# Up projection of an encoder layer: three seven-product row pairs per group in places three, five and seven, and TensorE in source order

## Chip, cores and metric

The kernel runs on one core of a Trainium2 chip, launched once. The metric is the device time of that core in microseconds (us). An execution's span, from its first to its last instruction in the profile, is given beside it.

Engines are named as in the profile: PE is TensorE (PEld its weight loads), DVE VectorE, ACT ScalarE, POOL GpSimd, SP SyncE. Each takes its own instructions in the order of its queue.

## What is computed

One layer of an encoder on 256 tokens of width 2048, in fp32. Two attention branches are gated, mixed and projected; then comes an MLP, and the change lies in its first half:

```
h = rms_norm(x, norm_mlp_pre)
u = square(relu(h @ w_up))        # 256 x 8192
x = x + rms_norm(u @ w_down, norm_mlp_post)
```

## The kernel before

Every fp32 operand is split into a high part, cast to the type fp32r, and a low part, the difference. A product of two such operands takes three matmuls: high by high, high by low, low by high.

The up projection goes over 8 groups of 1024 columns of `w_up`, u0 to u7 (the loop at L1141 and `wide_group`, L751). A group adds up 8 row pairs: pair i holds rows 256i to 256i + 255 of `w_up`, one load of 1 MB per group and pair (L651). The 256 tokens, the two halves of 128 rows of the pair and the two column halves make a product of 2 by 2 blocks. A plain pair computes it with eight block products, 24 matmuls of 128x512 (`eight`, L736). A heavy pair (`seven`, L724) uses a scheme of seven products, as Strassen's is, 21 matmuls. For that it needs sums of its weight blocks, t0 and t1 (DVE, L660 to L662), their high parts eh0 and eh1 (ACT, L672) and low parts el0 and el1 (DVE, L673), beside the split of three of its four blocks (h on ACT, L659, and l on DVE, L663). A plain pair has one cast of 2048 columns (ACT, L654) and one subtraction (DVE, L656). A heavy pair also needs sums of the stationary operand, `h2sum`, made once in group 0, which has plain pairs alone.

The table `UPS` (L1120) sets the order of the pairs in groups 1 to 7 and which are heavy. In this kernel pairs 3 and 5 are, in places four and six. Names tell group and pair: u3_5h is the high part of pair 5 in group 3. `Weights.next` (L687) prepares pairs two ahead of the one that PE works on. Raw, high and low parts have three buffers each, so a cast into one waits until PE has done with the pair three earlier; t0, t1 are in a pool of 27 pages, and the eh and el parts in a pool `mid`.

PSUM has eight banks. Four (the pool mm) hold products 1, 2, 3 and 7 of a group, to which plain pairs add. Four more (ms) go round among two users. The first are the transposes (`u_T`, L1092): the group before left two chunks of 512 columns, which 16 transposes (PE, L1100) turn, chunk by chunk at the second and third step of a group (n = 1, 2), each chunk in two banks, uT..0 and uT..1; ACT squares each bank into pages (L1103). The second are products 0, 4, 6 and 5, begun by a group's first heavy pair, which takes its products in the order 2, 1, 0, 4, 6, 5, 3. Of these, product 6 gets the bank of the odd chunk's uT..0 and product 5 that of its uT..1. The last heavy pair is followed by `combine` (L742), and the last plain pair by `u_piece` (L1114), which adds and applies ReLU and the row scale.

The squared chunks become stationary operands of the down projection (`u_sets`, `act_sets`, L1035): for an even chunk four sums sm (DVE, L1043 to L1046), then casts ah (ACT, L1058) and differences al (DVE, L1059), which POOL's queue writes to DRAM (L1062); for an odd chunk one cast and one difference. This stands at steps n = 6 and 7 of a group, in the last group at n = 1 and 2.

The instructions are put into each engine's queue by a scheduler that simulates the run. A dependence given by hand (`issue_after`) only orders the queues. `in_order` in `wide_group` does that for the matmuls of a group: each follows the one before it in the source. Here it is off in the up projection. `uw.behind` sets the weights prepared next behind the last addition of the group before.

Of the kernel before, what the change touches and what calls it, by code (L numbers as in the profile page):

```python
# [21 lines left out]
DFF = 4 * D  # L22
# [28 lines left out]
def encoder_layer(ctx: ExitStack, tc: tile.TileContext, a, out):  # L51
# [13 lines left out]
    def page(shape, dt, name):  # L65
        return pages.tile(shape, dt, tag="pg", name=name)
# [328 lines left out]
    late = {}  # L395
# [300 lines left out]
    def columns(src, i, c):  # L696
        return src[i * T : (i + 1) * T, c : c + 1024].rearrange("(k p) c -> p k c", p=P)
# [53 lines left out]
    def wide_group(name, kinds, weights, stat7, stat8, mm_banks, z, piece, each=None, turn=None, after={}, in_order=False):  # L751

        any7 = any(s for _, s in kinds)
        pr = Products(name, mm_banks)
        pr.in_order = in_order
        for n, (i, seven) in enumerate(kinds):
            w = weights.next(after)
            if each:  # L760
                each(n)
            if seven:
                final = not any(s for _, s in kinds[n + 1 :])
                pr.seven(partial(stat7, i), w, final)
                if final:
                    pr.combine(z)
                continue
            end = n == len(kinds) - 1
            if turn and n < 2:
                ahead = [*ahead, (i, w)] if n else [(i, w)]  # L770
                for t in range(2) if n else ():
                    for ii, ww in ahead:
                        for which in (2 * t, 2 * t + 1):
                            pr.eight(partial(stat8, ii), ww, which, False)
                    if not t:
                        turn()
                continue
            for which in range(4):
                pr.eight(partial(stat8, i), w, which, end)
                if end:  # L780
                    b, t, half = PLAIN[which]
                    piece(t, half, pr.ps[b], any7)

    def sums_of(p1, p2, name):

        a11, a21, a12, a22 = p1[:, :P], p1[:, P:], p2[:, :P], p2[:, P:]
        s = page([P, 4, P], F32, f"{name}s")
        nc.vector.tensor_sub(s[:, 0], a21, a22)
        nc.vector.tensor_sub(s[:, 1], a11, a21)
        nc.vector.tensor_sub(s[:, 2], s[:, 0], a11)  # L790
        nc.vector.tensor_add(s[:, 3], a12, s[:, 2])
        parts_ = page([P, 2, 4, P], F32R, name)
        nc.scalar.copy(parts_[:, 0], s)
        nc.vector.tensor_sub(parts_[:, 1], s, parts_[:, 0].bitcast(F32))
        return parts_
# [218 lines left out]
    def first_up(n):  # L1014
        for t, c in {2: [(1, 1), (0, 2)], 3: [(1, 2), (0, 3)], 4: [(1, 3)]}.get(n, ()):
            residual_parts(t, c)
        if n == 5:
            for t in range(2):
                mlp_squares(t)
                mlp_scale(t)  # L1020
            for i in range(4):
                kd = dram.tile([P, 1024], F32, name=f"keepx{i}", tag=f"keepx{i}")
                nc.gpsimd.dma_start(kd, x2[i])
                kept["x", i] = kd
# [10 lines left out]
    def act_sets(cg, u):  # L1035


        srcs = []
        if seven_of(cg):
            a11, a21 = u[:, 0:2, :P], u[:, 0:2, P:]  # L1040
            a12, a22 = u[:, 2:4, :P], u[:, 2:4, P:]
            sums = page([P, 4, 2, P], F32, f"sm{cg}")
            nc.vector.tensor_sub(sums[:, 0], a21, a22)  # L1043
            nc.vector.tensor_sub(sums[:, 1], a11, a21)
            nc.vector.tensor_sub(sums[:, 2], sums[:, 0], a11)
            nc.vector.tensor_add(sums[:, 3], a12, sums[:, 2])  # L1046
            own = [(slice(0, 1), a11.unsqueeze(1)),
                   (slice(1, 3), u[:, 2:4].rearrange("p k (t q) -> p t k q", t=2))]
            if cg in FIRST:
                own.append((slice(3, 4), a21.unsqueeze(1)))  # L1050
            srcs = [([P, 1 + len(own), 2, P], own), ([P, 4, 2, P], [(slice(0, 4), sums)])]
        else:
            srcs = [([P, 4, T], [(slice(0, 4), u)])]
        got = []
        for i, (shape, pieces) in enumerate(srcs):
            hi, lo = page(shape, F32R, f"ah{cg}{i}"), page(shape, F32R, f"al{cg}{i}")
            for at, src in pieces:
                nc.scalar.copy(hi[:, at], src)  # L1058
                nc.vector.tensor_sub(lo[:, at], src, hi[:, at].bitcast(F32))  # L1059
            for n, part in (("h", hi), ("l", lo)):  # L1060
                kd = dram.tile(shape, F32, name=f"keep{n}{cg}{i}", tag=f"keep{n}{cg}{i}")
                nc.gpsimd.dma_start(kd, part.bitcast(F32))  # L1062
                kept[cg, i, n] = (shape, kd)
            got.append([hi, lo])
        return got
# [26 lines left out]
    def u_T(cg, z):  # L1092

        u = page([P, 4, T], F32, f"u{cg}")
        for b in range(2):
            pt = bank(f"uT{cg}{b}")
            for j in range(2):
                for t in range(2):
                    c = (b * 2 + j) * P
                    nc.tensor.transpose(  # L1100
                        pt[:, j * T + t * P : j * T + (t + 1) * P], z[t][:, cg % 2, c : c + P], ident
                    )
            nc.scalar.activation(  # L1103
                u[:, b * 2 : b * 2 + 2], pt.rearrange("p (j q) -> p j q", j=2), AF.Square
            )
        return u

    def u_sets(cg, u):

        got = act_sets(cg, u)  # L1110
        if NG - 4 <= cg < NG - 2:
            sets[0, cg] = got
# [4 lines left out]
            uw.behind = nc.vector.tensor_add(zt, zt, ps).ins  # L1117
        nc.scalar.activation(zt, zt if summed else ps, AF.Relu, scale=r2[:, t : t + 1])

    UPS = [(0, 0), (1, 0), (2, 0), (3, 1), (4, 0), (5, 1), (6, 0), (7, 0)]  # L1120
    uw = Weights()
    for g in range(DFF // 1024):
        for i, seven in UPS if g else ALL8:
            uw.ask(columns(a["w_up"], i, g * 1024), f"u{g}_{i}", seven)
    wd = a["w_down"].rearrange("(g h j p) c -> p h g j c", h=2, j=2, p=P)

    blocks = [[NG - 4] + list(range(0, NG - 4, 2)) + [NG - 2], [NG - 2] + list(range(0, NG - 2, 2))]
# [12 lines left out]
    us = {}  # L1140
    for g in range(DFF // 1024):  # L1141
        z = Late(lambda g=g: [page([P, 2, 512], F32, f"u{g}{t}") for t in range(2)])

        def up_each(n, g=g, uz=uz):
            if not g:
                first_up(n)
                if n == 7:
                    for i in (3, 5):
                        f = page([P, 2, T], F32, f"h2f{i}")
                        for k in range(2):  # L1150
                            d = hT2[i][:, k].bitcast(F32)
                            nc.vector.tensor_add(f[:, k], d[:, :T], d[:, T:])
                        h2sum[i] = sums_of(f[:, 0], f[:, 1], f"h2s{i}")
                return
            cg = g * 2 - 3 + n
            if n in (1, 2):
                us[cg] = u_T(cg, uz)
            late = 0 if g == DFF // 1024 - 1 else 5
            if n - late in (1, 2):
                u_sets(cg - late, us[cg - late])  # L1160

        wide_group(
            f"u{g}",
            UPS if g else ALL8,
            uw,
            h2stat7,
            h2stat8,
            (1, 2, 3, 7),
            z,
            partial(u_piece, z=z),  # L1170
            each=up_each,
            turn=None if g else turn_rows,
            after={} if g else {1: tail[1][1], 2: scaled[0]},
        )
        uz = z

# [213 lines left out]
```

## Time and profile before

| what | value |
|---|---|
| time, median of three runs | 1351.32 us (1351.23 to 1351.63) |
| the profiled execution | 1352.06 us |
| its span | 1350.2 us |
| granted PE clock, mean | 0.998 |
| PE busy | 1337.3 us, 99% |
| DVE, ACT busy | 1029.6 us, 76%; 716.0 us, 53% |
| one group of the up projection (group 3) | 44.08 us |

A row of a timeline gives start, duration, engine, line, operation, output and inputs by name with their shapes, the number of instructions in the row, and in brackets the idle time ahead of it with what ended it. A row of the waits gives what waited, for whom, the total, how often and the longest. A row of the windows gives the stretch and its length, then for PE, PEld, DVE, ACT and POOL the busy time and instructions in it, then the granted clock, the DMA share and GB/s.

### The profile page before, as it was taken

The page shows a single profiled execution, that of the slowest core. Times are in us where ns is not written, and L with a number is a line of the kernel's source. Part 1 is how long each engine was busy: PE and PEld are TensorE (multiplying, and loading weights), DVE is VectorE, ACT ScalarE, POOL GpSimd, SP SyncE. Part 2 cuts the span into 40 slices and gives each one's busy share as a digit, 9 for nine tenths or more (in the row PEclk, how much of TensorE's full clock was granted, in tenths as well). Part 3 has the DMA queues.
Part 4 walks back from the last instruction along what each step waited for, and adds up shares of the span by engine and source line. Part 5 has one row for each costly group of instructions (what it writes and reads, how often), then busy time and mean ns, then how long its engine had stood idle before and what let it go on. Part 6 is the DMA issues. An engine that isn't in the chain of part 4 may idle for free.

```text
span 1350.2 us, 16169 instructions
## 1 busy us (share of the span) xinstructions
PE 1337.3 (99%) x6336; PEld 1118.8 (83%) x6336; DVE 1029.6 (76%) x1181; ACT 716.0 (53%) x841; POOL 38.5 (3%) x71
## 2 busy tenths in 40 slices
PE   9999999999999999999999999999999999999997
PEld 7888888888888888888788888888888888888885
DVE  6968866677857886654777788878888888798896
ACT  5755554544644454344575665666555545554552
POOL 0000000000000000000100000000000000000000
PEclk9999999999999999999999999999999999999999
DMA  9874755564556655575666777678799998798994
GB/s 323 278 220 162 204 163 181 184 183 156 189 187 216 218 187 187 198 270 192 216 204 221 250 273 271 231 234 279 265 339 329 364 359 337 276 357 331 363 360 192
DMA packets 116732, 335.85 MB, mean 249 GB/s; under 512 B 16944, under 2 KB 17712, under 8 KB 116656
## 3 DMA queue, kind: packets, MB, share of 16 engines
q1 hardware_dynamic: 97120, 266.12, 58.0%
q10 hardware_dynamic: 12816, 43.01, 8.3%
q0 software_dynamic: 6720, 25.69, 4.8%
q8 instruction: 49, 0.80, 0.2%
q14 instruction: 27, 0.22, 0.0%
HBM read 307.01 MB, written 29.61 MB: 249 GB/s over the span
## 4 chain that ended last, share of the span: by engine, by line
PE 97%; DVE 1%; DMA 1%; ACT 1%; issue 0%; DVEq 0%; POOLq 0%; POOL 0%; SPq 0%; ACTq 0%
PE u L718 25%; PE p L718 24%; PE ga L718 6%; PE gb L718 6%; PE ba L718 3%; PE bb L718 3%; PE qn_p L214 2%; PE kn_p L214 2%; PE y_p L259 2%; PE y_p L258 2%; PE y_p L257 2%; PE ka_p L214 2%; PE qa_p L214 2%; PE qn_p L216 1%; PE kn_p L216 1%; PE vn_p L258 1%
## 5 line engine op out<-in xcount | busy, mean ns | idle before, releaser
L138 DVE TENSOR_TENSOR y_l<-y_w,y_h 128x1024 fp32r<-128x1024 f32 x32 | 37.9, 1222 | 30.9 <-ACT y_h L133 30.9
L133 ACT CAST y_h<-y_w 128x1024 fp32r<-128x1024 f32 x32 | 32.0, 1051 | 40.9 <-PE y_p L259 32.5
L257 PE MATMUL y_p<-y_h,mh 128*128 128x512 f32 x128 | 50.1, 391 | 0.0
L258 PE MATMUL y_p<-y_l,mh 128*128 128x512 f32 x128 | 49.9, 390 | 0.0
L259 PE MATMUL y_p<-y_h,ml 128*128 128x512 f32 x128 | 49.8, 390 | 0.0
L214 PE MATMUL ka_p<-hT,ka_h 128*128 128x512 f32 x128 | 45.5, 399 | 0.6 <-DVE rope_s L284 0.6
L214 PE MATMUL qn_p<-hT,qn_h 128*128 128x512 f32 x128 | 45.8, 399 | 0.0
L214 PE MATMUL qa_p<-hT,qa_h 128*128 128x512 f32 x128 | 44.5, 403 | 0.8 <-DVE hT L298 0.8
L214 PE MATMUL kn_p<-hT,kn_h 128*128 128x512 f32 x128 | 45.3, 397 | 0.0
L718 PE MATMUL u<-u_0h,h2T 128*128 128x512 f32 x128 | 45.0, 396 | 0.0
L718 PE MATMUL u<-u_1h,h2T 128*128 128x512 f32 x128 | 43.7, 396 | 0.0
L718 PE MATMUL u<-u_2h,h2T 128*128 128x512 f32 x128 | 41.8, 396 | 0.0
L718 PE MATMUL u<-u_4h,h2T 128*128 128x512 f32 x128 | 41.2, 391 | 0.0
L718 PE MATMUL u<-u_6h,h2T 128*128 128x512 f32 x128 | 41.0, 389 | 0.0
L718 PE MATMUL u<-u_7h,h2T 128*128 128x512 f32 x128 | 40.9, 389 | 0.0
L656 DVE TENSOR_TENSOR u_7l<-u_7r,u_7h 128x2048 fp32r<-128x2048 f32 x8 | 18.3, 2293 | 28.1 <-ACT u_7h L654 28.1
L216 PE MATMUL qn_p<-hT,qn_l 128*128 128x256 f32 x128 | 35.9, 281 | 0.0
L216 PE MATMUL kn_p<-hT,kn_l 128*128 128x256 f32 x128 | 35.7, 280 | 0.0
L216 PE MATMUL ka_p<-hT,ka_l 128*128 128x256 f32 x128 | 35.2, 280 | 0.0
L216 PE MATMUL qa_p<-hT,qa_l 128*128 128x256 f32 x128 | 33.3, 282 | 0.4 <-DVE qa_l L138 0.3
L654 ACT CAST u_1h<-u_1r 128x2048 fp32r<-128x2048 f32 x8 | 15.3, 1914 | 33.6 <-PE u L718 29.6
L654 ACT CAST u_7h<-u_7r 128x2048 fp32r<-128x2048 f32 x8 | 15.3, 1914 | 31.8 <-issue 26.5
(1387 smaller groups left out, 4374.5 us busy)
## 6 DMA issues: line engine op xcount, KB each, us to landing
y_w<-in_w_out SPq DMA_DIRECT2D x16, 1024.0 KB, 5.1
bh<-keeph ACTq DMA_DIRECT2D x30, 512.0 KB, 9.8
bl<-keepl ACTq DMA_DIRECT2D x30, 512.0 KB, 11.5
keeph<-ah POOLq DMA_DIRECT2D x18, 512.0 KB, 6.3
keepl<-al POOLq DMA_DIRECT2D x18, 512.0 KB, 7.1
va_w<-in_w_in SPq DMA_DIRECT2D x8, 1024.0 KB, 5.1
qn_w<-in_w_in SPq DMA_DIRECT2D x8, 1024.0 KB, 5.1
kn_w<-in_w_in SPq DMA_DIRECT2D x8, 1024.0 KB, 5.1
```

What stands on the lines that cost most here:

```text
L133: nc.scalar.copy(hi[part], raw[part])
L138: sub = nc.vector.tensor_sub(lo[part], raw[part], hi[part].bitcast(F32)).ins
L214: nc.tensor.matmul(ps[b], hi[:, k % 4, cs], mv, start=(k == 0), stop=False)
L216: nc.tensor.matmul(ps[b][:, :T], lo[:, k % 4, cs], mv[:, :T], start=False, stop=(k == nk - 1))
L257: nc.tensor.matmul(ps[t], sh, hi[:, k % 4], start=(k == 0), stop=False)
L258: nc.tensor.matmul(ps[t], sh, lo[:, k % 4], start=False, stop=False)
L259: nc.tensor.matmul(ps[t], sl, hi[:, k % 4], start=False, stop=(k == nk - 1))
L654: nc.scalar.copy(h1, raw)
L656: nc.vector.tensor_sub(l1, raw, h1.bitcast(F32))
L718: ins = nc.tensor.matmul(self.ps[i], st, mv[:, blk], start=i not in self.begun, stop=last and n == 2).ins
```

## The change

Pair 0 becomes heavy too, and the pairs get a new order: 1, 2, 0, 4, 3, 6, 5, 7, with the heavy ones in places three, five and seven. The el parts go into pages instead of `mid`. In groups 1 to 7 PE's matmuls follow the source. The stationary sets move from steps n = 6 and 7 to n = 3 and 5, the fourth and the sixth step; the last group keeps n = 1 and 2. A third h2 sum is made.

```diff
-    UPS = [(0, 0), (1, 0), (2, 0), (3, 1), (4, 0), (5, 1), (6, 0), (7, 0)]
+    UPS = [(1, 0), (2, 0), (0, 1), (4, 0), (3, 1), (6, 0), (5, 1), (7, 0)]
...
-            uw.ask(columns(a["w_up"], i, g * 1024), f"u{g}_{i}", seven)
+            uw.ask(columns(a["w_up"], i, g * 1024), f"u{g}_{i}", seven, page)
...
-                    for i in (3, 5):
+                    for i in (0, 3, 5):
...
-            late = 0 if g == DFF // 1024 - 1 else 5
-            if n - late in (1, 2):
-                u_sets(cg - late, us[cg - late])
+            steps = (3, 5) if g < DFF // 1024 - 1 else (1, 2)
+            if n in steps:
+                cg = g * 2 - 2 + steps.index(n)
+                u_sets(cg, us[cg])
...
+            in_order=g > 0,
```

In the built program PE has 21 fewer matmuls of L718 (3 in each of groups 1 to 7), and as many transposes.

ACT in group 3, around the squares. Before: u4 and u5 are the even and the odd chunk, uT40 to uT51 their banks.

```order
L659 CAST u3_3h_6529<-u3_3r_6527 128x1536 [waits DMAHW7_49,PE_49,Activation_49]
L1103 ACTIVATE u4_6546<-uT40_6547 128x512 [waits PE_49]
L672 CAST u3_3eh1_6542<-u3_3t1_6532 128x1024 [waits DVE_49]
L1103 ACTIVATE u4_6546<-uT41_6553 128x512 [waits PE_49]
L654 CAST u3_4h_6585<-u3_4r_6583 128x2048 [waits DMAHW0_49,PE_49,Activation_49]
L1103 ACTIVATE u5_6589<-uT50_6590 128x512 [waits PE_49]
L1103 ACTIVATE u5_6589<-uT51_6596 128x512 [waits PE_49]
L672 CAST u3_5eh0_6637<-u3_5t0_6630 128x1024 [waits DVE_49]
```

Pair 3 is the first heavy pair here. Between the squares of the two chunks stand one eh cast and the cast of plain pair 4.

The same place after the change; u3_0 is now the first heavy pair, u3_3 the second, u3_6 the plain pair after it:

```order
L672 CAST u3_0eh1_6539<-u3_0t1_6529 128x1024 [waits DVE_49]
L1103 ACTIVATE u4_6577<-uT40_6578 128x512 [waits DMASW4_49,PE_49]
L1103 ACTIVATE u4_6577<-uT41_6584 128x512 [waits PE_49]
L659 CAST u3_3h_6616<-u3_3r_6614 128x1536 [waits DMAHW0_49,PE_49,Activation_49]
L672 CAST u3_3eh0_6625<-u3_3t0_6618 128x1024 [waits DVE_49]
L672 CAST u3_3eh1_6629<-u3_3t1_6619 128x1024 [waits DVE_49]
L654 CAST u3_6h_6673<-u3_6r_6671 128x2048 [waits DMAHW1_49,PE_49,Activation_49]
L1103 ACTIVATE u5_6633<-uT50_6634 128x512
L1103 ACTIVATE u5_6633<-uT51_6640 128x512
```

The squares of the odd chunk, u5, moved behind all three casts of u3_3 and that of u3_6.

PE in group 3 after the change, in the first heavy pair; u30, u34, u36 and u35 are products 0, 4, 6 and 5 of group 3:

```order
L718 MATMUL u30_6652<-u3_0h_6526,h2T0_4813 128x512 [waits Activation_49]
L718 MATMUL u30_6652<-u3_0l_6527,h2T0_4813 128x512
L718 MATMUL u30_6652<-u3_0h_6526,h2T0_4813 128x512
L718 MATMUL u34_6656<-u3_0eh0_6535,h2s0_5769 128x512 [waits Activation_49]
L718 MATMUL u34_6656<-u3_0el0_6536,h2s0_5769 128x512 [waits DVE_49]
L718 MATMUL u34_6656<-u3_0eh0_6535,h2s0_5769 128x512
L718 MATMUL u36_6660<-u3_0eh0_6535,h2s0_5769 128x512 [waits PE_49,Activation_49]
L718 MATMUL u36_6660<-u3_0el0_6536,h2s0_5769 128x512
L718 MATMUL u36_6660<-u3_0eh0_6535,h2s0_5769 128x512
L718 MATMUL u35_6664<-u3_0eh1_6539,h2s0_5769 128x512 [waits PE_49,Activation_49]
L718 MATMUL u35_6664<-u3_0el1_6540,h2s0_5769 128x512 [waits DVE_49]
L718 MATMUL u35_6664<-u3_0eh1_6539,h2s0_5769 128x512
```

Product 6 waits for ACT (the square of uT50, as the bank's user before it), as the 13th matmul after the last transpose; all later matmuls of the pair stand behind it. Before, plain pair 2 stood between the transposes and the first heavy pair.

ACT in group 1 after the change, around the squares of u1, the odd chunk:

```order
L672 CAST u1_3eh0_5925<-u1_3t0_5918 128x1024 [waits DVE_49]
L672 CAST u1_3eh1_5929<-u1_3t1_5919 128x1024 [waits DVE_49]
L659 CAST u1_3h_5916<-u1_3r_5914 128x1536 [waits DMAHW0_49,PE_49,Activation_49]
L1103 ACTIVATE u1_5933<-uT10_5934 128x512 [waits PE_49]
L1103 ACTIVATE u1_5933<-uT11_5940 128x512 [waits PE_49]
L1058 CAST ah00_5982<-u0_5877 128x256 [waits Activation_49]
L1058 CAST ah00_5982<-u0_5877 128x512 [waits Activation_49]
L654 CAST u1_6h_5973<-u1_6r_5971 128x2048 [waits DMAHW1_49,PE_49]
```

Here both eh casts of the second heavy pair stand ahead of u1_3h, and the squares ahead of u1_6h.

Group 7, the last, where the sets are made at the second and third step. Before, on PE, at the end of plain pair 4 (the place after the first heavy pair, u7_3); u76, u75 and u73 are products 6, 5 and 3:

```order
L718 MATMUL u73_7873<-u7_4h_7970,h2T4_4817 128x512 x2
L718 MATMUL u73_7873<-u7_4l_7971,h2T4_4817 128x512
L718 MATMUL u76_8052<-u7_3eh0_7898,h2s3_5769 128x512 [waits PE_49,Activation_49]
L718 MATMUL u76_8052<-u7_3el0_7899,h2s3_5769 128x512
L718 MATMUL u76_8052<-u7_3eh0_7898,h2s3_5769 128x512
L718 MATMUL u75_8056<-u7_3eh1_7902,h2s3_5769 128x512 [waits PE_49,Activation_49]
L718 MATMUL u75_8056<-u7_3el1_7903,h2s3_5769 128x512
L718 MATMUL u75_8056<-u7_3eh1_7902,h2s3_5769 128x512
L718 MATMUL u73_7873<-u7_4h_7970,h2T4_4817 128x512
```

Products 6 and 5 of heavy pair 3 had been put behind nearly all of plain pair 4; in the changed program they stand in their own pair, as in group 3.

After the change, on ACT, from the squares of chunk 12 (even) to those of chunk 13 (odd):

```order
L1103 ACTIVATE u12_7977<-uT120_7978 128x512 [waits PE_49]
L1103 ACTIVATE u12_7977<-uT121_7984 128x512 [waits PE_49]
L1058 CAST ah120_7995<-u12_7977 128x256 [waits Activation_49]
L1058 CAST ah120_7995<-u12_7977 128x512 [waits Activation_49]
L1058 CAST ah120_7995<-u12_7977 128x256
L659 CAST u7_3h_8041<-u7_3r_8039 128x1536 [waits DMAHW0_49,PE_49]
L654 CAST u7_6h_8106<-u7_6r_8104 128x2048 [waits DMAHW1_49,PE_49]
L1058 CAST ah121_8007<-sm12_7990 128x1024 [waits DVE_49]
L672 CAST u7_3eh0_8050<-u7_3t0_8043 128x1024 [waits DVE_49]
L672 CAST u7_3eh1_8054<-u7_3t1_8044 128x1024 [waits DVE_49]
L1103 ACTIVATE u13_8058<-uT130_8059 128x512
L1103 ACTIVATE u13_8058<-uT131_8065 128x512
```

The squares of uT130 and uT131 now stand behind the ah casts of chunk 12, u7_3h, u7_6h and both eh casts.

After the change, on DVE, at the same place:

```order
L663 TENSOR_TENSOR u7_3l_8042<-u7_3r_8039,u7_3h_8041 128x1536 [waits DMAHW0_49,Activation_49]
L1046 TENSOR_TENSOR sm12_7990<-u12_7977,sm12_7990 128x256 [waits DVE_49]
L656 TENSOR_TENSOR u7_6l_8107<-u7_6r_8104,u7_6h_8106 128x2048 [waits DMAHW1_49,Activation_49]
L1059 TENSOR_TENSOR al121_8008<-sm12_7990,ah121_8007 128x1024 [waits Activation_49]
L660 TENSOR_TENSOR u7_3t0_8043<-u7_3r_8039 128x1024 [waits DMASW6_49]
L661 TENSOR_TENSOR u7_3t1_8044<-u7_3t0_8043,u7_3r_8039 128x512 [waits DVE_49]
L662 TENSOR_TENSOR u7_3t1_8044<-u7_3t1_8044,u7_3r_8039 128x512 [waits DVE_49]
L673 TENSOR_TENSOR u7_3el0_8051<-u7_3t0_8043,u7_3eh0_8050 128x1024 [waits DMASW7_49,Activation_49]
L673 TENSOR_TENSOR u7_3el1_8055<-u7_3t1_8044,u7_3eh1_8054 128x1024 [waits Activation_49]
L1059 TENSOR_TENSOR al130_8072<-u13_8058,ah130_8071 128x1024 [waits Activation_49]
```

The sums t0 and t1 of u7_3, from which ACT casts eh0 and eh1, stand behind u7_6l and al121.

## Prediction

> **What bounds the kernel now.** I read the page's first and fourth parts, then the list of waits on TensorE (PE) from 640 us to the end, then one whole group of the up projection (group 3) in the windows and the timeline.
>
> ```profile
> span 1350.2 us, 16169 instructions
> PE 1337.3 (99%) x6336; PEld 1118.8 (83%) x6336; DVE 1029.6 (76%) x1181; ACT 716.0 (53%) x841; POOL 38.5 (3%) x71
> PE 97%; DVE 1%; DMA 1%; ACT 1%; issue 0%; DVEq 0%; POOLq 0%; POOL 0%; SPq 0%; ACTq 0%
> PE u L718 <- DVE u_1l L656: 0.8, 1, 0.8
> 788.58:832.66 44.08, 44.08 (x203) 36.48 (x202) 35.71 (x35) 25.94 (x26) 3.23 (x7) 1.00 0.75 257
> ```
>
> PE is busy for 99% of the span and makes 97% of the chain that ends last. The fourth row is all that PE waits from 640 us on: one wait of 0.8, in group 0. The fifth is group 3 from its first matmul to that of group 4: 44.08 us, PE busy in all of it, DVE for 35.71, ACT for 25.94, granted clock 1.00. So a matmul saved here is time saved, and a wait added is time added, with nothing on PE to hide it.
>
> ```profile
> 811.59 0.39 PE L718 MATMUL u<-u_4h,h2T 128*128 128x512 f32 x1
> 817.03 0.39 PE L718 MATMUL u<-u_5h,h2s 128*128 128x512 f32 x1
> 821.79 0.39 PE L718 MATMUL u<-u_6h,h2T 128*128 128x512 f32 x1
> ```
>
> These are the first matmuls of a plain pair, of the heavy pair behind it and of the next plain pair. Matmuls overlap, so their cost is the distance of starts: 24 take 817.03 − 811.59 = 5.44, 21 take 4.76, 0.2267 each. Group 3 has 6 × 24 + 2 × 21 = 186 matmuls, 42.17; the 16 transposes take the other 44.08 − 42.17 = 1.91.
>
> **The change part by part.** *Matmuls removed.* A third heavy pair takes 3 matmuls from each of groups 1 to 7: 21 × 0.2267 = 4.76 us, all of it on the path.
>
> *What the third heavy pair adds on DVE and ACT.* Beside a plain pair it adds these and drops one cast and one subtraction:
>
> ```profile
> 817.27 1.91 ACT L654 CAST u_7h<-u_7r 128x2048 fp32r<-128x2048 f32 x1 [5.29 <-issue]
> 819.22 2.29 DVE L656 TENSOR_TENSOR u_7l<-u_7r,u_7h 128x2048 fp32r<-128x2048 f32 x1 [4.40 <-ACT u_7h L654]
> 808.59 1.76 DVE L663 TENSOR_TENSOR u_5l<-u_5r,u_5h 128x1536 fp32r<-128x1536 f32 x1 [1.67 <-ACT u_5h L659]
> 991.21 1.22 DVE L660 TENSOR_TENSOR u_5t<-u_5r 128x1024 f32<-128x1024 f32 x1
> 992.47 0.69 DVE L661 TENSOR_TENSOR u_5t<-u_5t,u_5r 128x512 f32<-128x512 f32 x1
> 993.19 0.69 DVE L662 TENSOR_TENSOR u_5t<-u_5t,u_5r 128x512 f32<-128x512 f32 x1
> 993.80 1.22 DVE L673 TENSOR_TENSOR u_5el<-u_5t,u_5eh 128x1024 fp32r<-128x1024 f32 x1
> ```
>
> DVE: 1.76 + 1.22 + 2 × 0.69 + 2 × 1.22 − 2.29 = 4.5 more, 40.2 of a group's 43.4 without waits. ACT gains one cast of 1.48 and two of 1.05 (rows below) and loses 1.91: 27.6. Both fit, so I cost them at nothing; what it costs where the cover fails is the fourth rival. The third h2 sum is made once, in group 0, and the low parts in pages take the same time in another buffer.
>
> *The places and the order.* Here lies the cost. The transposes of the group before (uT) take the four ms banks of PSUM, two at each of the second and third steps, and ACT's squares (L1103) empty them. The next users are products 0, 4, 6, 5 of the group's first heavy pair, so product 6 waits for the square of the third step's first bank. Before, this pair is the fourth, and a plain pair lies between. Now it is third: its product 6 stands 12 matmuls behind the last transpose, and as PE's order is that of the source, whatever it waits for stops all that follows.
>
> How late is that square? The order of ACT (in the part on the change) puts it behind u3_3h, two eh casts and u3_6h. The times come from these rows:
>
> ```profile
> 797.37 0.40 PE L718 MATMUL u<-u_0h,h2T 128*128 128x512 f32 x1
> 797.85 1.48 ACT L659 CAST u_3h<-u_3r 128x1536 fp32r<-128x1536 f32 x1 [3.98 <-PE u L718]
> 799.23 0.59 ACT L1103 ACTIVATE u<-uT 128x512 f32<-128x512 f32 x1
> 799.72 1.04 ACT L672 CAST u_3eh<-u_3t 128x1024 fp32r<-128x1024 f32 x1
> 800.66 0.60 ACT L1103 ACTIVATE u<-uT 128x512 f32<-128x512 f32 x1
> 801.15 1.91 ACT L654 CAST u_4h<-u_4r 128x2048 fp32r<-128x2048 f32 x1
> 802.95 1.09 ACT L1103 ACTIVATE u<-uT 128x512 f32<-128x512 f32 x2
> ```
>
> u_3h's cast waits for the last matmul that reads the buffer it goes into, and starts 0.48 behind that matmul's start. From start to start the casts take 1.38 (L659), 0.94 (L672) and 1.80 (L654); a square lasts 0.59.
>
> Groups 2 to 6, clock at 0 with the group's first matmul: two plain pairs and the transposes end at 2 × 5.44 + 1.91 = 12.8, and product 6 is due 12 × 0.2267 later, at 15.52. The last matmul of the second pair, u_2, starts before the eight late transposes: 12.8 − 0.95 − 0.23 = 11.62. ACT starts u3_3h at 12.10 and ends the square at 12.10 + 1.38 + 2 × 0.94 + 1.80 + 0.59 = 17.75. PE follows 0.05 later:
>
> ```profile
> 654.75 2.28 DVE L656 TENSOR_TENSOR u_1l<-u_1r,u_1h 128x2048 fp32r<-128x2048 f32 x1
> 657.08 0.50 PE L718 MATMUL u<-u_1l,h2T 128*128 128x512 f32 x1 [0.85 <-DVE u_1l L656]
> 657.42 0.62 PE L718 MATMUL u<-u_1h,h2T 128*128 128x512 f32 x2
> ```
>
> (654.75 + 2.28 = 657.03, then 657.08.) The wait is 17.80 − 15.52 = 2.28, in five groups 11.4. It is at least 1.85 if the cast follows its matmul at 0.05 instead of 0.48, and at most 3.4 if DVE's sums hold the eh casts for one L660 (1.22) more; I take the 0.48, since that row shows this very wait. The restart costs too: the second matmul came 0.34 after the first instead of 0.227, 0.11 for each wait.
>
> Group 1: the order has ACT's late squares ahead of u1_6h and its eh casts early, so the squares end near 14.4, before 15.5: no wait.
>
> Group 7: the order keeps the sets at the second and third steps. There ACT does the early squares, ah casts, u7_3h, u7_6h, ah, both eh casts and only then the late squares; the second eh cast needs DVE's L662, and that stands behind u7_6l and al121.
>
> ```profile
> 1024.43 1.22 DVE L1059 TENSOR_TENSOR al<-sm,ah 128x1024 fp32r<-128x1024 f32 x1
> 1025.57 1.22 DVE L660 TENSOR_TENSOR d000t<-d000r 128x1024 f32<-128x1024 f32 x1
> 811.40 2.29 DVE L656 TENSOR_TENSOR u_6l<-u_6r,u_6h 128x2048 fp32r<-128x2048 f32 x1
> 813.60 1.22 DVE L673 TENSOR_TENSOR u_5el<-u_5t,u_5eh 128x1024 fp32r<-128x1024 f32 x1
> ```
>
> u7_6h takes the buffer of u7_0h, read last by the heavy pair's ninth matmul, which starts at 12.8 + 8 × 0.2267 = 14.61; so ACT starts it at 15.09 and it ends at 17.00. DVE starts u7_6l 0.04 later, as 819.22 follows 817.27 + 1.91. Then 2.20 (start to start, 811.40 to 813.60) and 1.14 for al121 (1024.43 to 1025.57) end at 20.38. L660 and L661 take 1.26 and 0.72 (991.21, 992.47, 993.19), L662 0.69: 23.05. ACT's second eh cast follows at 23.10, the square at 24.04, ending 24.63; PE goes on at 24.68. Product 6 was due at 15.52: a wait of 9.16.
>
> That PE used to have the freedom that the change takes away can be seen in group 7 of before, where the squares end at 984.95 + 1.08 = 986.03:
>
> ```profile
> 984.95 1.08 ACT L1103 ACTIVATE u<-uT 128x512 f32<-128x512 f32 x2
> 985.88 0.39 PE L718 MATMUL u<-u_3eh,h2T 128*128 128x512 f32 x1
> 990.42 0.39 PE L718 MATMUL u<-u_3eh,h2s 128*128 128x512 f32 x1
> ```
>
> Product 3 was taken at 985.88, and products 6 and 5 only at 990.42, behind most of the next plain pair.
>
> *The sum.* −4.76 + 11.4 + 9.16 + 6 × 0.11 = +16.5. The profiled execution took 1352.06 (its span 1350.2 and 1.86 around it): 1368.6. The median is 0.74 below that execution, so I forecast **1367.8**.
>
> **The rivals.** *The clock.* After the pause of 9 us PE might run slowly for a while. The nearest rows are the kernel's first matmuls and the same form a little later:
>
> ```profile
> 5.51 1.64 PE L214 MATMUL qa_p<-hT,qa_h 128*128 128x512 f32 x4 [0.30 <-DVE hT L298]
> 7.46 1.08 PE L214 MATMUL qa_p<-hT,qa_h 128*128 128x512 f32 x4
> ```
>
> By them it costs 0.56 more: 1368.4. The Trainium skill, "TensorE: Matmul & The Clock Gate" (Part 1, and the closing table), says that an idle window of about 3.4 us puts the clock back to half until about 3.4 us of work have passed; by that page I estimate 1.7 more, 1369.5. No run here shows which: the trace has no pause of that length within the work.
>
> *Group 7 waits only as the others do* (DVE makes its sums earlier than the order says): 2.28 in place of 9.16 gives 1360.9. Against it: engines take their rows in order, and L662 stands behind u7_6l.
>
> *The other side: the squares come in time.* If ACT reached them by 15.5 − 5.65 = 9.8 instead of 12.10, that is if u_3h's buffer came free a pair earlier, no wait is left, only the 4.76 saved: 1351.32 − 4.76 = 1346.6. It decides at 2.28 less on ACT's chain in groups 2 to 6. Against it speaks 797.85, where this very cast waits on PE for 3.98.
>
> *DVE becomes the bound.* Its idle time per group before is 44.08 − 35.71 = 8.4. If it is all unavoidable (waits on ACT), a group needs 40.2 + 8.4 = 48.6 instead of the forecast's 44.08 − 0.68 + 2.28 + 0.11 = 45.8: 5 × 2.8 = 14 more, 1382. Against it: much of that idle time is DVE waiting for buffers that PE holds.
>
> That nothing changes can be left out: the order shows 21 matmuls fewer.
>
> **How the numbers follow.** Forecast 0.64, at 1365.6 to 1373.4 (five waits of 1.85 or 3.4); clock 0.15; group 7 like the others 0.10; squares in time 0.07; DVE 0.04. The range goes from 1358.7 (group 7 like the others, with the low waits) to 1373.4. A difference of 0.2%, 2.7 us, is about what a measurement of this kernel can tell from no change. Faster by more: the squares in time, 0.06, and 0.02 within; slower the rest, 0.92.
>
> **What would show it.** In the list of waits, matmuls of u that wait for ACT's squares, L1103: five times about 2.3 and once about 9.2. Group windows of about 45.8 (groups 2 to 6), 43.4 (group 1) and 52.7 (group 7), with the clock at 1.00. The down projection as long as before. I am wrong if the product behind the eh matmuls of the first heavy pair follows at 0.23, or if PE waits for DVE's el parts rather than for ACT.

## The result and the profile after

The changed kernel took 1377.28 us (median of 4 runs, 1376.14 to 1377.45) against 1351.47 before: 25.8 us slower; over all runs the ratio is 1.0186 (95% interval 1.0173 to 1.0199). The forecast was 1367.8 with a range to 1373.4, so the direction was right, the size too small, and the time lies above the range. The profiled execution took 1377.42, its span 1375.6.

The page of the changed kernel, and below it all waits of PE from 640 us on:

```profile
span 1375.6 us, 16212 instructions
PE 1342.9 (98%) x6315; PEld 1121.9 (82%) x6315; DVE 1060.9 (77%) x1223; ACT 727.1 (53%) x856; POOL 38.5 (3%) x71
PE 95%; ACT 2%; DVE 1%; DMA 1%; SPq 0%; issue 0%; DVEq 0%; POOLq 0%; POOL 0%; ACTq 0%
```

```profile
PE u L718 <- ACT u L1103: 19.7, 6, 8.9
PE u L718 <- DVE u_1l L656: 0.8, 1, 0.8
```

The six forecast waits for ACT's squares are there, 19.7 us in all, and no other wait is new. They account for most of the loss but not for all of it. And PE is busy for 5.6 us *more* than before, 1342.9 against 1337.3, though it has 21 matmuls fewer. Something made matmuls longer. The six places in the timeline of PE:

```profile
761.64 0.50 PE L718 MATMUL u<-u_0eh,h2s 128*128 128x512 f32 x1 [2.15 <-ACT u L1103]
807.46 0.50 PE L718 MATMUL u<-u_0eh,h2s 128*128 128x512 f32 x1 [2.16 <-ACT u L1103]
854.89 0.51 PE L718 MATMUL u<-u_0eh,h2s 128*128 128x512 f32 x1 [2.16 <-ACT u L1103]
902.34 0.50 PE L718 MATMUL u<-u_0eh,h2s 128*128 128x512 f32 x1 [2.15 <-ACT u L1103]
949.76 0.50 PE L718 MATMUL u<-u_0eh,h2s 128*128 128x512 f32 x1 [2.16 <-ACT u L1103]
1003.97 0.80 PE L718 MATMUL u<-u_0eh,h2s 128*128 128x512 f32 x1 [8.93 <-ACT u L1103]
```

ACT ahead of the second of them:

```profile
801.74 1.48 ACT L659 CAST u_3h<-u_3r 128x1536 fp32r<-128x1536 f32 x1 [2.55 <-issue]
803.12 2.00 ACT L672 CAST u_3eh<-u_3t 128x1024 fp32r<-128x1024 f32 x2
805.02 1.89 ACT L654 CAST u_6h<-u_6r 128x2048 fp32r<-128x2048 f32 x1
806.82 1.07 ACT L1103 ACTIVATE u<-uT 128x512 f32<-128x512 f32 x2
```

The two squares, in one row here, stand behind the four casts, and PE goes on at 807.46, 17.79 after the group's start at 789.67 (forecast: 17.80).

The waits are equal in groups 2 to 6, but the stretches between them are not: 45.82 from the first to the second, then 47.43, 47.45, 47.42. The windows of the groups say where that comes from (groups 2, 3, 4, 7 and the down projection; after the busy times comes the granted clock):

```profile
743.85:789.67 45.82, 43.66 (x201) 35.91 (x199) 39.89 (x41) 27.30 (x27) 3.23 (x6) 1.00 0.71 246
789.67:837.10 47.43, 45.27 (x200) 37.04 (x199) 39.85 (x41) 27.32 (x27) 3.23 (x6) 0.96 0.68 240
837.10:884.55 47.45, 45.29 (x201) 37.06 (x199) 39.86 (x41) 27.30 (x27) 3.23 (x6) 0.96 0.68 239
...
979.40:1034.46 55.06, 46.13 (x200) 37.70 (x199) 40.67 (x42) 28.20 (x28) 3.19 (x6) 0.91 0.64 225
1034.46:1375.60 341.14, 331.86 (x1472) 274.68 (x1470) 281.00 (x250) 171.68 (x146) 4.60 (x8) 0.99 0.85 326
```

Group 2 ran at a clock of 1.00, groups 3 to 6 at 0.96, group 7 at 0.91. In group 3, right behind the pause:

```profile
807.80 0.55 PE L718 MATMUL u<-u_0el,h2s 128*128 128x512 f32 x1
808.15 1.05 PE L718 MATMUL u<-u_0eh,h2s 128*128 128x512 f32 x2
809.00 0.63 PE L718 MATMUL u<-u_0el,h2s 128*128 128x512 f32 x1
809.43 0.63 PE L718 MATMUL u<-u_0eh,h2s 128*128 128x512 f32 x1
...
810.71 0.63 PE L718 MATMUL u<-u_0eh,h2T 128*128 128x512 f32 x1
811.13 0.48 PE L718 MATMUL u<-u_4h,h2T 128*128 128x512 f32 x1
811.45 0.40 PE L718 MATMUL u<-u_4l,h2T 128*128 128x512 f32 x1
```

From start to start a matmul takes 0.43 instead of 0.227, until 811.13, and then it is back. Against a group with the same pause and the full clock (group 2) that costs 47.43 − 45.82 = 1.61.

| part of the sum | forecast | measured |
|---|---|---|
| matmuls saved (group 1: 43.40) | −4.76 | −4.76 |
| waits of groups 2 to 6 | 5 × 2.28 = 11.4 | 5 × 2.16 = 10.8 |
| wait of group 7 | 9.16 | 8.93 |
| restarts | 0.66 | 5 × (45.82 − 43.40 − 2.15) + 0.11 = 1.46 |
| slow clock, groups 3 to 6 | 0 | 4 × 1.61 = 6.44 |
| slow clock, group 7 | 0 (as a rival 0.56) | 55.06 − 43.40 − 8.93 − 0.11 = 2.62 |
| down projection | 0 | 341.14 − 341.20 = −0.06 |
| sum | 16.5 | 25.4 |

The last column meets the difference of the spans, 1375.6 − 1350.2 = 25.4.

The row of the restarts holds more than a restart. The forecast counted a wait from the time when the product was due to start, the profile counts idle time from the end of the matmul before. A matmul starts 0.227 after the one before it but lasts 0.39, so the profile's wait is 0.16 shorter. In the forecast's terms the waits were 2.32 and 9.09, and the matmul behind a wait came 0.11 late, both nearly as forecast. The same 0.16 is in the 2.62 of group 7, which leaves 2.46 for the clock there.

### The profile page after: what moved, and what is told of

It is laid out like the page before. It is cut to its first block, busy times and chain, and to the rows that moved or that the text cites. A ratio compares the mean times of both kernels' runs of the same rounds, so it can differ in the third digit from the quotient of the medians.

```text
span 1375.6 us, 16212 instructions
## 1 busy us (share of the span) xinstructions
PE 1342.9 (98%) x6315; PEld 1121.9 (82%) x6315; DVE 1060.9 (77%) x1223; ACT 727.1 (53%) x856; POOL 38.5 (3%) x71
## 4 chain that ended last, share of the span: by engine, by line
PE 95%; ACT 2%; DVE 1%; DMA 1%; SPq 0%; issue 0%; DVEq 0%; POOLq 0%; POOL 0%; ACTq 0%
PE u L718 25%; PE p L718 24%; PE ga L718 6%; PE gb L718 6%; PE ba L718 3%; PE bb L718 3%; PE ka_p L214 2%; PE qn_p L214 2%; PE kn_p L214 2%; PE y_p L258 2%; PE y_p L259 2%; PE y_p L257 2%; PE qa_p L214 1%; PE qn_p L216 1%; PE ka_p L216 1%; PE kn_p L216 1%
## 5 line engine op out<-in xcount | busy, mean ns | idle before, releaser
L718 PE MATMUL u<-u_2h,h2T 128*128 128x512 f32 x128 | 43.4, 401 | 0.0
L718 PE MATMUL u<-u_4h,h2T 128*128 128x512 f32 x128 | 43.3, 408 | 0.0
L718 PE MATMUL u<-u_1h,h2T 128*128 128x512 f32 x128 | 41.4, 392 | 0.0
L718 PE MATMUL u<-u_6h,h2T 128*128 128x512 f32 x128 | 40.7, 390 | 0.0
L718 PE MATMUL u<-u_7h,h2T 128*128 128x512 f32 x128 | 40.7, 389 | 0.0
L718 PE MATMUL u<-u_0eh,h2s 128*128 128x512 f32 x42 | 18.2, 467 | 19.7 <-ACT u L1103 19.7
L1118 ACT ACTIVATE u<-u,r 128x512 f32<-128x512 f32 x32 | 21.5, 713 | 28.3 <-DVE u L1117 26.8
L656 DVE TENSOR_TENSOR u_1l<-u_1r,u_1h 128x2048 fp32r<-128x2048 f32 x8 | 18.3, 2290 | 20.3 <-ACT u_1h L654 20.3
L718 PEld LDWEIGHTS u<-u_4h,h2T 128*128 128x128 f32 x128 | 25.9, 203 | 5.8
```

What stands on the lines that cost most here:

```text
L656: nc.vector.tensor_sub(l1, raw, h1.bitcast(F32))
L718: ins = nc.tensor.matmul(self.ps[i], st, mv[:, blk], start=i not in self.begun, stop=last and n == 2).ins
```

## The experiments

Two things were to be told apart: whether PE's waits come from ACT's queue as the order has it, and whether the slow matmuls come from the pauses or from something else that three heavy pairs bring (DVE at 40 us per group). Unless something else is said, an edit is made to the changed kernel. Times are medians; each is set against runs of the kernel before on the same chip.

**Only the squares' place on ACT** (sq_first). The names between u2_6 and u6_6 are left out here. The added lines shift later ones by three: L721 and L1106 are L718 and L1103.

```diff
+    last_sq = [None]
...
-            nc.scalar.copy(h1, raw)
+            with tc.issue_after(last_sq[0]) if name in ("u2_6", ..., "u6_6") else nullcontext():
+                nc.scalar.copy(h1, raw)
...
-            nc.scalar.activation(
+            last_sq[0] = nc.scalar.activation(
                 u[:, b * 2 : b * 2 + 2], pt.rearrange("p (j q) -> p j q", j=2), AF.Square
-            )
+            ).ins
```

> The changed kernel with one thing moved on ACT: in groups 2 to 6 the cast of the plain pair 6 (L654) is put behind the odd chunk's two squares. Theory (PE waits for the squares as ACT's queue has them, and the clock falls where over about 1.75 us of a window of 3.4 us are idle): the squares come 1.80 sooner, the five waits fall from 2.16 to 0.36, the clock stays up in these groups, each takes 44.0, and the time is 1377.3 - 5 x 1.80 - 4 x 1.61 = 1361.9, with group 7 as it was. Rival (the wait is for something else that ends at the same time, such as u_6's cast or el1 on DVE): waits of 2.2 stay, 1377. Rival (the clock is lowered by a wait of any length): 1368.

Measured: 1361.96 (ratio to before 1.0078, 1.0064 to 1.0092). Ahead of product 6 only the cast u_6h moved, behind the squares; farther on in the group u_7h also moved, ahead of the eh casts of u_5, without a wait of PE. PE's waits:

```profile
759.21 0.50 PE L721 MATMUL u<-u_0eh,h2s 128*128 128x512 f32 x1 [0.35 <-ACT u L1106]
803.22 0.50 PE L721 MATMUL u<-u_0eh,h2s 128*128 128x512 f32 x1 [0.36 <-ACT u L1106]
...
987.84 0.79 PE L721 MATMUL u<-u_0eh,h2s 128*128 128x512 f32 x1 [8.93 <-ACT u L1106]
```

The waits are 1.80 shorter, which is one cast of 2048 columns, and groups 2 to 6 take 44.0 each. Both the wait's cause and the sum of wait and clock stand as the theory had them.

**Work in place of the pause** (fill). Groups 2 to 6 compute product 4 of the first heavy pair three more times, to no use.

```diff
+            if 4 not in self.begun and self.name in ("u2", "u3", "u4", "u5", "u6"):
+                for _ in range(3):
+                    self.add(4, stat(3), t[0], 0, True)
+                    self.begun.discard(4)
             self.add(4, stat(3), t[0], 0, last)
```

> In groups 2 to 6 the first heavy pair computes its product 4 four times (three times to no use), 9 more matmuls, 2.04 us, ahead of product 6; so PE works through most of its pause of 2.16. Theory (the slow clock comes from the pause): no slow matmuls in these groups, each 45.7 us, about 6.5 us less in all though nothing is saved: 1370 to 1371. Rival (matmuls there are slow for another reason, such as what ACT and DVE do at that time): groups of 47.4 as now, 1377.

Measured: 1371.53 (1.0142, 1.0128 to 1.0156), though PE has 45 matmuls more. Two of its groups:

```profile
744.49:790.30 45.81, 45.69 (x209) 37.58 (x208) 39.89 (x41) 27.32 (x27) 3.22 (x6) 1.00 0.70 245
790.30:836.13 45.83, 45.70 (x209) 37.58 (x208) 39.85 (x41) 27.33 (x27) 3.23 (x6) 1.00 0.71 249
```

Groups 3 to 6 fell from 47.43 to 45.83, the clock is 1.00, and DVE and ACT are as busy as they were (39.9 and 27.3). So it is the pause that lowers the clock, not the load beside it.

**A shorter pause** (p3_first).

```diff
-            self.add(6, stat(4), t[0], 1, last)
-            self.add(5, stat(5), t[1], 0, last)
-            self.add(3, stat(2), t[1], 1)
+            if self.name[0] == "u":
+                self.add(3, stat(2), t[1], 1)
+            self.add(6, stat(4), t[0], 1, last)
+            self.add(5, stat(5), t[1], 0, last)
+            if self.name[0] != "u":
+                self.add(3, stat(2), t[1], 1)
```

> Product 3 is put ahead of products 6 and 5, so these are due 0.68 later, and the pauses are 1.48 in groups 2 to 6 and 8.25 in group 7. Theory (the clock is lowered where about 1.9 us or more of a window of 3.4 us are idle): the short pauses leave the clock at 1.00, groups 2 to 6 take 45.1, and the time is 1377.3 - 6 x 0.68 - 4 x 1.63 = 1366.7. Rival (any pause costs the clock some 1.6 us in four groups of five): 1373.2. Rival (slow clock in proportion to the pause): 1371.

Measured: 1367.37 (1.0112, 1.0098 to 1.0125). The five pauses for the squares (L1106 here) are 1.48 and cost no clock; a group is 45.13:

```profile
761.42 0.50 PE L718 MATMUL u<-u_0eh,h2s 128*128 128x512 f32 x1 [1.48 <-ACT u L1106]
806.54 0.50 PE L718 MATMUL u<-u_0eh,h2s 128*128 128x512 f32 x1 [1.48 <-ACT u L1106]
```

0.68 less of waiting saved 2.3 in each of groups 3 to 6. A cost in proportion to the pause is out, and so is a cost of any pause.

**Group 7's sets later** (sets7).

```diff
-            steps = (3, 5) if g < DFF // 1024 - 1 else (1, 2)
+            steps = (3, 5)
```

> The changed kernel, with the sets of the last group at the fourth and sixth step as in the others. Theory (the long wait of group 7 is u7_6l and al121 standing ahead of the sums on DVE): ACT's order becomes that of groups 2 to 6, the wait there falls from 8.9 to 2.2, group 7 takes 47.4 (45.8 if the clock stays up) in place of 55.1, and the time is 1377.3 - 7.6 = 1369.7 (1368.1). Rival (the sets, now later, hold up the start of the down projection): group 7 shorter, but a wait of PE for ah or al at its first matmuls, 1372 or more.

Measured: 1369.87 (1.0133, 1.0119 to 1.0147). The wait of group 7 falls from 8.93 to that of the others, and the group takes 47.41:

```profile
951.67 0.50 PE L718 MATMUL u<-u_0eh,h2s 128*128 128x512 f32 x1 [2.16 <-ACT u L1103]
997.48 0.60 PE L718 MATMUL u<-u_0eh,h2s 128*128 128x512 f32 x1 [2.16 <-ACT u L1103]
```

So the early sets of the last group are what made its wait long. The down projection was hardly held up by the later ones: its only wait is 0.2 us, on a load of a kept low part. This run also has six equal pauses, of which five were followed by slow matmuls (all but that of 951.67).

**Source order alone, in the kernel before** (b_inorder).

```diff
             after={} if g else {1: tail[1][1], 2: scaled[0]},
+            in_order=g > 0,
```

> The kernel before with in_order in groups 1 to 7 and nothing else. Theory (source order costs only where a matmul is late, and a plain pair stands between the transposes and the first heavy pair here): no more than 0.3 us in group 7, 1351 to 1353. Rival (source order costs in itself, by taking from PE the filling of small gaps): 1355 or more, spread over all groups.

Measured: 1354.72 against 1351.81 (1.0023, 1.0014 to 1.0032). Neither theory had this. Groups 1 to 6 take 44.0 to 44.1 as before, so nothing is spread; but in group 7 one wait came up:

```profile
998.81 0.51 PE L718 MATMUL u<-u_5el,h2s 128*128 128x512 f32 x1 [1.84 <-DVE u_5el L673]
```

That is 1.84 and not the 0.3 that I allowed: with PE in source order, the second heavy pair's el part is late there. On ACT and DVE the cast and the subtraction of plain pair u_7 stand ahead of its eh cast and of the el part itself (u_7l from 995.33 for 2.29 us, u_5el from 997.54 for 1.22), and on DVE the sums of u_5 stand behind u_6l and an al of the sets. Which of these matters most was not tried in this kernel. The profiled span is 2.0 longer than that of before; the rest of the 2.9 between medians isn't explained.

**PE's order left to the scheduler** (free_order).

```diff
-            in_order=g > 0,
```

> The changed kernel without in_order in the up projection; the scheduler is free to put products 6 and 5 later. Theory: the squares are as late as they were, but no matmul stands behind them, so PE does not wait in groups 2 to 6, and under 1 us in group 7: 1346.7 to 1347.7. Rival (three heavy pairs cost more in themselves): 1351 or more, with waits on DVE.

Measured: 1351.41 (0.9994, 0.9985 to 1.0003), as the kernel before. Groups 1 to 6 took 43.3 each with no wait: although the squares are behind the same casts, products 6 and 5 stand farther back. Group 7 took 47.43, with a slow stretch at half clock and, ahead of it, two waits that the theory did not have:

```profile
1001.76 0.50 PE L718 MATMUL u<-u_5eh,h2s 128*128 128x512 f32 x1 [0.68 <-ACT u_5eh L672]
1004.28 0.50 PE L718 MATMUL u<-u_5el,h2s 128*128 128x512 f32 x1 [1.79 <-DVE u_5el L673]
```

The time did not reach the 1346.7 that I gave. The next run asks whether the sets of the last group are the reason.

**The two together** (free_sets7): without `in_order`, and `steps = (3, 5)` in every group.

> free_order with the sets of the last group at the fourth and sixth step. Theory: without them ahead, the sums and eh casts of u7_5 come in time, the two waits of 0.7 and 1.8 in group 7 and the slow clock behind them go, and group 7 takes 43.3 in place of 47.4: 4 us less than free_order, 1347.4. Rival (the loss moves on to the start of the down projection): 1351 as free_order.

Measured: 1349.03 (0.9978, 0.9969 to 0.9987), faster than the kernel before. All seven groups take 43.3, so group 7 gave back its 4.2. Of the gain, part went to the rival's place: the down projection is 345.16 long, against 343.55 in free_order and 341.20 in the kernel before, with 2.4 us of waits on loads of kept low parts that the kernel before does not have. The other 1.6 of these 4.0 isn't explained.

```profile
PE p L718 <- DMA bl<-keepl: 2.4, 3, 1.6
```

**Both chunks transposed at the second step** (t_early), in source order.

```diff
-            cg = g * 2 - 3 + n
-            if n in (1, 2):
-                us[cg] = u_T(cg, uz)
+            if n == 1:
+                for cg in (g * 2 - 2, g * 2 - 1):
+                    us[cg] = u_T(cg, uz)
```

> Both chunks are transposed at the second step of a group, so that ACT's squares stand ahead of u3_3h and u3_6h; all else is as in the changed kernel. Theory (all of the loss is PE's wait for the squares and the slow clock behind these pauses): no wait on L1103 is left, groups of 43.4 us, granted clock 1.00, and the time is that of the kernel before less 4.76: 1346.7. Rival (three heavy pairs cost more in themselves, by DVE's 40 us of work per group): PE waits for el parts or sums in place of squares, groups of 44 us or more, 1351 to 1377.

Measured: 1356.64 (1.0032, 1.0021 to 1.0043): a miss for the theory as stated. No wait for squares is left, but in groups 2, 4 and 6 another has come, and one in group 7:

```profile
783.60 0.50 PE L718 MATMUL u<-u_5el,h2s 128*128 128x512 f32 x1 [1.88 <-DVE u_5el L673]
874.12 0.50 PE L718 MATMUL u<-u_5el,h2s 128*128 128x512 f32 x1 [1.88 <-DVE u_5el L673]
963.04 0.50 PE L718 MATMUL u<-u_5el,h2s 128*128 128x512 f32 x1 [1.88 <-DVE u_5el L673]
997.36 0.50 PE L718 MATMUL u<-u_3el,h2s 128*128 128x512 f32 x1 [0.88 <-DVE u_3el L673]
```

ACT and DVE of this run, ahead of the first of these:

```profile
778.17 1.91 ACT L654 CAST u_1h<-u_1r 128x2048 fp32r<-128x2048 f32 x1 [3.61 <-PE u L718]
779.99 1.04 ACT L672 CAST u_5eh<-u_5t 128x1024 fp32r<-128x1024 f32 x1
```

```profile
777.33 0.68 DVE L662 TENSOR_TENSOR u_5t<-u_5t,u_5r 128x512 f32<-128x512 f32 x1
780.12 2.29 DVE L656 TENSOR_TENSOR u_1l<-u_1r,u_1h 128x2048 fp32r<-128x2048 f32 x1 [2.10 <-ACT u_1h L654]
782.33 1.22 DVE L673 TENSOR_TENSOR u_5el<-u_5t,u_5eh 128x1024 fp32r<-128x1024 f32 x1
```

The sum was ready at 778.0; ACT could not cast it, since the next group's u_1h stood ahead of it and waited 3.61 for PE to give a buffer free (and on DVE u_1l stood ahead of u_5el). The first of PE's four waits also lowered the clock: group 2 took 47.24, groups 4 and 6 took 45.7. In groups 3 and 5 the two casts stand the other way round, with no wait and 43.25 per group. This is the first fault again, a cast that waits for PE ahead of one that PE waits for, and not DVE's load.

**That order mended** (early_eh): t_early, `steps = (3, 5)`, and plain pairs' casts behind the last eh cast made before them.

```diff
+    last_eh = [None]
...
-            nc.scalar.copy(h1, raw)
+            with tc.issue_after(last_eh[0]) if last_eh[0] and name[0] == "u" else nullcontext():
+                nc.scalar.copy(h1, raw)
...
-            nc.scalar.copy(h2[i], t[i])
+            last_eh[0] = nc.scalar.copy(h2[i], t[i]).ins
```

> t_early, with plain pairs' casts (L654) put behind the last eh cast of the heavy pair ahead of them, and the sets of the last group at the fourth and sixth step. Theory (what t_early lost in groups 2, 4 and 6 is u_5's second eh cast standing on ACT behind the next group's u_1h, which waits for PE): no waits of 1.9 on u_5el, groups of 43.3, 1346.7 to 1348. Rival (DVE's 40 us per group leave no room, so another el part or sum comes late in its place): 1351 or more.

Measured: 1348.69 (0.9978, 0.9969 to 0.9987). Groups 1 to 7 take 43.3, with no wait of PE in them. Three heavy pairs do fit, then, and the rival on DVE's load falls; the time is a little over the theory's 1348.

**The same with PE's order free** (early_eh_free): without `in_order` as well.

> early_eh with the order of PE left to the scheduler. Theory (no matmul is late there any more, so source order costs nothing): the same groups of 43.3, 1348 to 1349.5, no better than early_eh. Rival (source order costs in itself): 1 us or more less than early_eh, 1347.5 or below.

Measured: 1347.65 (0.9970, 0.9960 to 0.9981), the fastest of all, with the same groups of 43.2 to 43.3 and the same span of 1345.9 as early_eh. The spans say that source order costs nothing there; the medians are 1.0 apart, but come from two different chips, and don't settle it.

## Why the prediction was wrong

*What bounds the kernel, the matmuls saved.* Right: every wait added shows in full, and group 1, the one without a wait, takes 43.40 as forecast.

*The places and the order.* Right in mechanism, place and size: five waits of 2.16 of idle time (2.32 from the due start) against 2.28, one of 8.93 (9.09) against 9.16, and none in group 1. sq_first moved the one cast and the wait went down by its 1.80; sets7 took the sets away and group 7's wait became that of the others.

*What three heavy pairs add on DVE and ACT, at nothing.* Right for this kernel; the busy time is 39.9 and 27.3 against the forecast's 40.2 and 27.6. The cover is thinner than I made it where the order is bad: t_early, free_order and, with two heavy pairs, b_inorder each show an el part that comes 1.8 to 1.9 late.

*The clock.* This is the step that failed: the sum put the clock at nothing behind all six pauses. The prediction had a slow clock as a rival, after the pause of 9 us alone, at 0.56 from the kernel's first matmuls. It came after that pause at 2.62, and after four of the five pauses of 2.2 at 1.61 each: 9.1 us that the sum left out, and without which it would have been within 0.3 of what was measured (16.5 − 0.85 for shorter waits + 0.8 for longer restarts, against 25.4 − 9.1). For the pauses of 2.2 the prediction gave no reason to put it at nothing. Its one reading was the granted clock of 1.00 in group 3 of the kernel before, and that kernel has no pause over 0.85 from 640 us on, so its profile could say nothing on such pauses.

The Trainium skill, "TensorE: Matmul & The Clock Gate" (Part 1), gave a half clock for about 3.4 us, which I estimated at 1.7, for the pause of 9 us alone. That size agrees with the 1.61 measured behind each of four shorter pauses. Its condition, a whole idle window of about 3.4 us, does not: 2.16 was enough in four groups of five, so the measurement decides.

*The range* ended at 1373.4 since it took in the bounds of the waits and not that of the clock for each of them: five more times 1.6 would have put its upper end at 1381. (A small slip besides: 2.28 + 1.22 is 3.50, not 3.4.)

*The rivals* on group 7, on squares in time and on DVE as the bound did not come.

## What to carry to other kernels

Where PE is the bound and its order is fixed, look on each helper engine's queue for an instruction that waits for PE and stands ahead of one that PE waits for; each such pair can be a stall, and moving one cast took 1.80 away five times. Price a new PE pause at more than its length: here 2.16 of waiting cost up to 2.16 + 0.27 + 1.61, and cutting it to 1.48 saved 2.3 where the clock had fallen. Saved matmuls (4.76) were there all along: with the queues mended the same three heavy pairs came out 3.1 to 4.3 us, 0.2 to 0.3%, faster than the kernel before.

## What the runs showed of the hardware

A pause of PE of about 2 us can halve the granted clock for 3.4 us after it (0.43 per matmul of 128x512 instead of 0.227). Pauses of 1.48 never did (five of five), those of 1.79 to 1.88 in two cases of five (free_order once; t_early in group 2, not in 4 and 6; not in b_inorder), those of 2.16 in nine of eleven (four of five in the changed kernel, five of six in sets7), those of 8.3 to 8.9 in all four runs that were looked at for it, for 10.2 us that begin within the pause.

The slow stretches do not begin at a fixed time behind the pause: 0.44 after it in group 3 of the changed kernel, 1.50 after it in group 6. They keep a grid, which the granted clock of its trace shows. Stretches of groups 3, 4 and 7:

```profile
807.90:811.30 3.40, 3.40 (x10) 2.62 (x9) 3.40 (x5) 0.80 (x2) 0.54 (x1) 0.50 0.77 295
811.31:855.68 44.37, 42.21 (x194) 34.70 (x193) 36.79 (x37) 26.86 (x27) 2.69 (x5) 1.00 0.68 236
855.69:859.09 3.40, 3.40 (x9) 2.65 (x8) 3.40 (x5) 0.45 (x1) 0.54 (x1) 0.50 0.77 266
999.05:1009.28 10.23, 5.31 (x13) 4.16 (x14) 9.26 (x11) 5.17 (x6) 1.59 (x3) 0.50 1.00 354
```

The clock is 0.50 or 1.00 in the whole of each row. The slow stretches of groups 3 to 7 begin at 807.90, 855.68, 903.47, 951.26 and 999.04, each 47.79 after the one before, which is 14 × 3.413; the first four last 3.41, the last 10.24, which is 3 × 3.413. So the clock changed only at the ends of windows of about 3.413 us, wherever PE's pauses lay. By this grid the pause of group 2, 759.48 to 761.64, is cut at 760.11 into 0.63 and 1.53, and no slow stretch followed. That of group 6, 947.60 to 949.76, is cut at 947.84 into 0.24 and 1.92, and the clock fell at that window's end, 951.26. Those of groups 3 to 5 lie whole in one window each.

The two closest cases are the sixth group of sets7 and group 7 of free_order, one window and the next of each:

```profile
949.96:953.36 3.40, 1.69 (x7) 1.42 (x8) 3.40 (x5) 2.96 (x5) 0.15 (x1) 1.00 0.90 296
953.37:956.77 3.40, 3.40 (x16) 2.82 (x15) 2.60 (x5) 0.77 (x1) 0.93 (x2) 1.00 0.72 233
```

```profile
1001.98:1005.38 3.40, 1.61 (x7) 1.00 (x7) 2.50 (x3) 0.21 (x1) 0.00 (x0) 1.00 0.96 373
1005.39:1008.79 3.40, 3.40 (x10) 2.66 (x9) 3.37 (x6) 0.74 (x1) 0.00 (x0) 0.50 1.03 419
```

With 1.72 of a window idle the clock stayed up, with 1.79 it fell. A threshold between these two, on the idle time within one window, gives the outcome of all 21 pauses of 1.48 to 2.16 counted above. That the clock goes by this idle time is an inference from them: pauses of chosen length at chosen places were not tried, and idle time is counted here from the modelled ends of matmuls.
